# Attention stage: both query roundings ahead of both subtractions, the halves of a transposed pair laid one behind the other, reciprocal and scaling as a stage of their own

## Chip, cores and metric

The kernel runs on one core of a Trainium2 chip, in one launch. The metric is the device time of one execution in microseconds. "Before" ran three times; the median is 2232.25 us. One further execution was profiled, and the durations quoted here come from it.

## What is computed

One step of a two-layer encoder for a prompt of 1024 rows and a sample of 32 rows, with 1024 features in float32. Layer 0 is an mLSTM mixer with a SwiGLU feed-forward part, layer 1 is windowed attention with a second feed-forward part. Only the attention of layer 1 is touched by the change. Its reference, cut to what matters:

```python
def sink_attention(q, k, v, sinks, bias):
    s = jnp.einsum('bcqhgd,bckhd->bchgqk', q, k).astype(F32) * (HEAD_DIM ** -0.5) + bias
    sk = sinks.astype(F32).reshape(N_KV_HEADS, GROUP)[:, :, None, None]
    mx = jnp.maximum(jnp.max(s, -1, keepdims=True), sk)
    p = jnp.exp(s - mx)
    p = p / (jnp.sum(p, -1, keepdims=True) + jnp.exp(sk - mx))
    return jnp.einsum('bchgqk,bckhd->bcqhgd', p.astype(v.dtype), v)
```

There are 16 query heads of 64 features and 2 key/value heads. A query chunk of 64 rows sees 192 keys: its own chunk and the two before it. The sample sees 128 cached keys and its own 32. Each head has a learned sink, which enters the maximum and the sum and has no value row.

## The kernel before

**Number format.** TensorE multiplies in a rounded format. So an operand x is kept as two parts: hi, which ScalarE (ACT in the profile) makes by a rounding copy, and lo = x - hi, which VectorE (DVE) or GpSimd (POOL) makes by a subtraction. A dense product (`gemm`, L400 to L411) takes three products for each block of 128 features: hi by hi (L408), hi by lo (L409), lo by hi (L410). Dense weights are loaded by SyncE's queue, cast by ACT (L240) and subtracted by POOL or DVE (L242). The activations are split in L438 and L439, the tiles being `sx`.

**Order.** The order of issue is written out by hand. The dense products are the main thread. After each block of three products `wv.tick(us)` advances the clock of the scheduler by the estimated time of the block, and each generator whose pause has run out is pushed on to its next `yield`; what it issues then stands in the engines' queues between the dense products. `wv.drain` pushes one generator on without any dense products between. Every engine works through its own queue in order, so an instruction that has to wait holds all that is queued behind it.

**Queries.** `q_group(j, g)` (L1662) projects the query heads 2j and 2j+1 for a group g of 384, 384 or 288 columns into one PSUM bank (tile `d`; partitions 0 to 63 are one head, 64 to 127 the other). It then scales and splits them into the tile `Q`. For each half i, ACT rounds the half into its own partitions (L1677), and DVE subtracts: scaled source minus rounded value (L1678), with the result on the other 64 partitions. So in `Q` a column holds hi of a head on one half of the partitions and lo on the other. In the group of 288 columns this is done twice, for 256 and for 32 columns.

**Attention.** `attention` (L1778) goes over 72 items (j, b): 8 pairs of query heads and 9 blocks b of the sequence (8 of the prompt, 128 query rows each, and the sample as block 8). `pipeline` (L105) carries each item through stages, each of them a function with a lag and a pause:

- `scores` (L1790): four products (two in block 8) into `psS` (L1807); DVE adds the bias and takes the running minimum into the tile `s` and into `st` (L1813). Signs are turned around, so a minimum serves as the maximum.
- `soft` (L1821): ACT takes the exponential with its sum (L1828), DVE the reciprocal of the sum (L1833), POOL multiplies the probabilities by it (L1836; L1840 in the blocks 0 and 8).
- `turn` (L1850), lag 1: PE transposes the probabilities into the PSUM tile `T` (L1861); ACT rounds them into `hi` (L1865) and DVE subtracts into `lo` (L1866). Two successive items, j even and j odd, share one pair of tiles `hi`, `lo`. In blocks 0 and 8 this is done in two cuts.
- `values` (L1868), lag 1: on the odd item of a pair, up to eight products with the values into `O` (L1890).
- `place` (L1892): ACT copies the lower half of `O` (L1904) and DVE adds both halves into the activations `act` (L1908).

A stage with lag 1 takes an item only when the stage before it is two items ahead; with lag 0, one item. In each turn of its loop, `pipeline` looks at the stages in the order 4, 2, 3, 1, 0 (place, turn, values, soft, scores) and issues one item of each that may go. `turn` and `scores` pause for `GAP_A` = 0.46 us, the odd `values` for 0.92 us.

**Around it.** The first four query groups are projected while the layer normalisation before them still runs; then the values of the first group are transposed (L1762) and split (`VR`, L1691, L1692). While the attention runs, the main thread projects the other query groups; it waits with ticks of 0.25 us where the scores are too far behind (L1954). From the third column group on, it multiplies the finished part by the output weights (`out_tile`, L1237). `before(0)` (L1945) drains the attention generator up to the end of the first column group, `finish` (L1976) to its end. `mixed_parts` (L1205) splits the finished activations.

Of the kernel before, what the change touches and what calls it, by code (L numbers as in the profile page):

```python
# [9 lines left out]
F32 = mybir.dt.float32  # L10
F32R = mybir.dt.float32r
AF = mybir.ActivationFunctionType
ALU = mybir.AluOpType
# [3 lines left out]
P = 128  # L17
# [3 lines left out]
DEC = 32  # L21
# [264 lines left out]
def kernel(ctx: ExitStack, tc: tile.TileContext, A, O):  # L286
    nc = tc.nc
# [5 lines left out]
    def pool(name, space=None, side=None):  # L293
        kw = {}
        if space is not None:
            kw["space"] = space
        if side is not None:
            kw["side"] = side
        return tc.tile_pool(name=name, bufs=1, reuse_waits="tile", **kw)

    def new(p, tag, shape, dt=F32, bufs=1):
        uid[0] += 1
        return p.tile(list(shape), dt, name=f"{tag}_{uid[0]}", tag=tag, bufs=bufs)
# [20 lines left out]
    for j in range(PAIRS):  # L324
        U_Q.append(add("wqk", 2 * j))
        U_K.append(add("wqk", 2 * j + 1))
        v = ("wv", 2 * j - 2) if j else ("wvg", 0)
# [103 lines left out]
    def project(u, g):  # L431

        ps = psdense(g)
        gemm(ps, wcols(u), xcols(g))
        return ps
# [1226 lines left out]
    def q_group(j, g):  # L1662

        t0, n = GRP[g]
        ps = project(U_QB[g > 0][j], g)
        q = Q[j, g] = new(pb, "Q", [P, 2 * 384], F32R, bufs=4)
        sc = -(HD ** -0.5)
        for a, w in ((0, LC), (LC * (n // LC), n % LC)):
            m = n // LC * LC if w == LC else w
            if not m:  # L1670
                continue
            src = ps[:, a : a + m].rearrange("p (c w) -> p c w", w=w)
            dst = q[:, 2 * a : 2 * a + 2 * m].rearrange("p (c h w) -> p c h w", h=2, w=w)
            for i in range(2):
                own, other = slice(64 * i, 64 * i + 64), slice(64 - 64 * i, 128 - 64 * i)
                h = dst[own, :, i]
                nc.scalar.activation(h, src[own], AF.Copy, scale=sc)  # L1677
                nc.vector.scalar_tensor_tensor(  # L1678
                    dst[other, :, i], src[own], sc, h.bitcast(F32), op0=ALU.mult, op1=ALU.subtract
                )  # L1680

    ck = new(pb, "ck", [P, P])
# [44 lines left out]
    for j in range(4):  # L1727
        q_group(j, 0)
        W.done(U_QB[0][j])
# [13 lines left out]
    pb2 = eb.enter_context(pool("pb2"))  # L1743
# [34 lines left out]
    def attention(gap):  # L1778
        S, pairs_ = {}, {}

        def parts(b):

            if b == 0:
                return [(0, 400, 130, 64, 0, 1 + P), (1, 258, 258, P, 0, 1 + LC)]
            if b == 8:
                return [(0, 2, 2, P + DEC, SEQ, 1)]
            k0 = (b - 1) * P
            return [(0, 2, 2, WK, k0, 1), (1, 2 + WK, 2 + WK, WK, k0 + LC, 1)]
# [32 lines left out]
        def soft(j, b):  # L1821
            s = S[j, b]
            p, st = s["p"], s["st"]
            rows = 2 * DEC if b == 8 else P
            for c, _, at, nk, _, _ in parts(b):
                first = b != 0 and c == 0
                cols = slice(at - first, at + nk + (not first))
                nc.scalar.activation(  # L1828
                    p[:rows, cols], p[:rows, cols], AF.Exp, bias=st[:rows, 0, c : c + 1], scale=-1.0,
                    accum_out=st[:rows, 1, c : c + 1],  # L1830
                )
            n = len(parts(b))
            nc.vector.reciprocal(st[:rows, 2, :n], st[:rows, 1, :n])  # L1833
            if 0 < b < 8:
                w = p[:, 2 : 2 + 2 * WK].rearrange("p (c k) -> p c k", c=2)
                nc.gpsimd.tensor_mul(w, w, st[:, 2].unsqueeze(2).broadcast_to([P, 2, WK]))  # L1836
            else:
                for c, _, at, nk, _, _ in parts(b):
                    w = p[:rows, at : at + nk]
                    nc.gpsimd.tensor_scalar_mul(w, w, st[:rows, 2, c : c + 1])  # L1840

        def blocks(b):

            if b == 0:
                return [(1, 130, 64), (2, 258, P)]
            if b == 8:
                return [(0, 2, P), (1, 130, DEC)]
            return [(t, 2 + t * P, P) for t in range(3)]

        def turn(j, b):  # L1850
            s = S.pop((j, b))
            p = s["p"]
            rows = 2 * DEC if b == 8 else P
            if j % 2 == 0:
                pairs_[j // 2, b] = {
                    tag: new(pb2, tag, [P, 3, 2, P], F32R, bufs=2) for tag in ("hi", "lo")
                }
            s = pairs_[j // 2, b]
            pt = new(psb, "T", [P, 512], bufs=2).rearrange("p (t r) -> p t r", t=4)
            for t, at, nk in blocks(b):  # L1860
                nc.tensor.transpose(pt[:nk, t, :rows], p[:rows, at : at + nk], ident[:rows, :rows])  # L1861
            cuts = [(slice(0, 3), P)] if 0 < b < 8 else [(slice(t, t + 1), nk) for t, _, nk in blocks(b)]
            hi, lo = (s[x][:, :, j % 2, :] for x in ("hi", "lo"))
            for t, nk in cuts:
                nc.scalar.copy(hi[:nk, t, :rows], pt[:nk, t, :rows])  # L1865
                nc.vector.tensor_sub(lo[:nk, t, :rows], pt[:nk, t, :rows], hi[:nk, t, :rows].bitcast(F32))  # L1866

        def values(j, b):  # L1868

            if j % 2 == 0:  # L1870
                return
            s = pairs_[j // 2, b]
            g2 = j // 4
            po = s["po"] = new(psb, "O", [P, 2, 2, P])
            full = lambda i: VR[:, i, g2].rearrange("p a d -> p (a d)")
            if b == 0:
                sums = [[(1, full(0), 64)], [(2, full(0), P)]]
            elif b == 8:
                sums = [[(0, full(9), P), (1, full(8), DEC)]]
            else:  # L1880
                sums = [
                    [(0, full(b - 1), P), (1, VZ[0][:, b], P)],
                    [(1, VZ[1][:, b - 1], P), (2, full(b), P)],
                ]
            rows = 2 * DEC if b == 8 else P
            for c, terms in enumerate(sums):
                out = po[:, c, :, :rows]
                todo = [(v, s[x][:nk, t, :, :rows], nk) for t, v, nk in terms for x in ("hi", "lo")]
                for i, (v, x, nk) in enumerate(todo):
                    nc.tensor.matmul(out, v[:nk], x, start=i == 0, stop=i == len(todo) - 1)  # L1890

        def place(j, b):  # L1892
# [12 lines left out]
            for h in range(2):  # L1905
# [4 lines left out]
        always = lambda j, b: True  # L1910
# [3 lines left out]
            [  # L1914
                (scores, lambda j, b: ast["ready"] > QG.index((j, CH[b][3])), 0, (gap,) * 8),
                (soft, always, 0, 0),
                (turn, always, 1, (gap,) * 8),
                (values, lambda j, b: ast["v"] > b, 1, (0.0, 2 * gap) * 4),
                (place, always, 0, 0),
            ],  # L1920
            (4, 2, 3, 1, 0),
        )


    for t in spread:
        wv.drain(t)
    wv.launch(v_turn(0, 0))
    task = wv.launch(attention(GAP_A))
    ast["ready"] = 4
    for g in range(1, 3):  # L1930
# [20 lines left out]
    for n, (jp, g) in enumerate(JG):  # L1951
        if n < 2:
            continue
        while ast["scored"] < 6 * (n - 1):  # L1954
            wv.tick(0.25)
        for j in (2 * jp, 2 * jp + 1):
            q_group(j, g)
            wv.launch(q_made())
            if g != 1:
                W.done(U_QB[g > 0][j])  # L1960
        if n == 3:
            nparts[0] = 0
            parts = wv.launch(
                mixed_parts(
                    scr,
                    lambda g: ast["ready"] > QG.index((7, g)),
                    lambda k, g: ast["placed"] >= last_item(k, g),
                    (1.6, 1.0, 1.0),
                )
            )  # L1970
        if g == 2 and jp < EARLY:
            before(0)
            out_tile(U_OUT_B[0][jp], jp, QUARTERS[0][0])
            W.done(U_OUT_B[0][jp])
# [140 lines left out]
```

## Time and profile before

| | us |
|---|---|
| median of 3 runs (lowest, highest) | 2232.25 (2231.88, 2234.61) |
| profiled execution, device time | 2232.42 |
| its span, first to last instruction | 2230.6 |
| attention products, first to last (L1807 to L1890) | 1211.1 to 1443.9 |

The span is cut by the page into 40 slices of 55.8 us; the attention fills slices 22 to 26. A row of a group of instructions names line, engine, operation, tile written and tiles read, form and count; then the busy time, the mean of one, and the idle time of the engine ahead of them with what ended it. In the lists of waits "A <- B" says that A's engine stood idle until B had finished. PE is TensorE, PEld its weight load.

### The profile page before, as it was taken

What the parts mean: (1) busy time and instruction counts of PE and PEld (TensorE: products, weight loads), DVE (VectorE), ACT (ScalarE), POOL (GpSimd) and SP (SyncE); (2) the same over time, 40 slices, a digit from 0 to 9 for tenths busy, and PEclk for the clock granted to TensorE, in tenths of its full rate; (3) what the DMA queues carried; (4) which work ended last, traced back from release to release, by engine and by line L of the source; (5) the groups of instructions that cost most, each with busy time, mean ns of one, the idle gap of its engine ahead of it and who ended that gap; (6) DMA issues with size and microseconds to landing.
All of it is one profiled execution on the core that took longest, in us unless ns stands there. A gap on an engine that the chain in (4) does not pass through costs nothing.

```text
span 2230.6 us, 43755 instructions
## 1 busy us (share of the span) xinstructions
PE 2176.4 (98%) x16982; PEld 2143.3 (96%) x16982; DVE 1444.7 (65%) x2812; ACT 1006.7 (45%) x2263; POOL 952.6 (43%) x976
## 2 busy tenths in 40 slices
PE   9999999999999999999998989899999999999997
PEld 9999999999999999999997888799999999999997
DVE  4465677787666655566577666788765666466657
ACT  4444455374444443322246767756444444432125
POOL 2544210004655555544435645400565555554441
PEclk9999999999999999999999999999999999999999
DMA  5221213212434433896524311321344334397722
GB/s 169 77 61 56 57 39 100 75 39 97 156 144 154 145 126 125 308 303 214 162 70 124 100 57 55 99 82 39 106 165 155 138 143 155 124 338 264 236 65 78
DMA packets 166192, 289.97 MB, mean 130 GB/s; under 512 B 16416, under 2 KB 121944, under 8 KB 165984
## 3 DMA queue, kind: packets, MB, share of 16 engines
q1 hardware_dynamic: 161632, 282.84, 37.9%
q10 hardware_dynamic: 4352, 4.33, 0.6%
q8 instruction: 134, 2.20, 0.4%
q14 instruction: 74, 0.61, 0.1%
HBM read 202.35 MB, written 82.94 MB: 128 GB/s over the span
## 4 chain that ended last, share of the span: by engine, by line
PE 83%; DVE 8%; ACT 5%; DMA 2%; issue 1%; POOL 1%; SPq 0%; ACTq 0%; DVEq 0%; POOLq 0%
PE d L408 9%; PE A L408 9%; PE d L410 9%; PE A L410 9%; PE A L409 9%; PE d L409 9%; PE B L408 7%; PE B L409 7%; PE B L410 7%; PE O L1890 1%; ACT s L1828 1%; ACT act L511 1%; DVE Q L1678 1%; DMA hs_x<-z 1%; DMA sx<-hs_t 1%
## 5 line engine op out<-in xcount | busy, mean ns | idle before, releaser
L242 POOL TENSOR_TENSOR wl_s<-wr,wh_s 128x512 fp32r<-128x512 f32 x224 | 304.5, 1369 | 237.0 <-ACT wh_s L240 175.6
L408 PE MATMUL d<-sx,wh 128*128 128x264 f32 (+2 forms) x1048 | 338.4, 323 | 4.1 <-ACT wh L240 4.0
L242 POOL TENSOR_TENSOR wl_a<-wr,wh_a 128x512 fp32r<-128x512 f32 x112 | 153.3, 1372 | 413.4 <-ACT wh_a L240 409.6
L410 PE MATMUL d<-sx,wl 128*128 128x264 f32 (+2 forms) x1048 | 321.6, 307 | 4.2 <-DVE wl L242 2.8
L409 PE MATMUL d<-sx,wh 128*128 128x264 f32 (+2 forms) x1048 | 321.3, 307 | 0.4 <-DVE sx L439 0.4
L408 PE MATMUL A<-sx,wh_s 128*128 128x264 f32 x896 | 254.5, 284 | 0.0
L409 PE MATMUL A<-sx,wh_s 128*128 128x264 f32 x896 | 254.2, 284 | 0.0
L410 PE MATMUL A<-sx,wl_s 128*128 128x264 f32 x896 | 254.0, 283 | 0.0
L240 ACT CAST wh_s<-wr 128x512 fp32r<-128x512 f32 x224 | 135.7, 617 | 192.5 <-DVE wr L195 102.6
L408 PEld LDWEIGHTS d<-sx,wh 128*128 128x128 f32 x1048 | 199.5, 190 | 7.4 <-ACT wh L240 4.3
L410 PEld LDWEIGHTS d<-sx,wl 128*128 128x128 f32 x1048 | 198.8, 190 | 5.5 <-DVE wl L242 3.3
L409 PEld LDWEIGHTS d<-sx,wh 128*128 128x128 f32 x1048 | 199.8, 191 | 1.5 <-DVE sx L439 0.7
L408 PE MATMUL d<-sx,ex 128*128 128x264 f32 x624 | 180.6, 289 | 0.1
L409 PE MATMUL d<-sx,ex 128*128 128x264 f32 x624 | 177.2, 284 | 0.0
L410 PE MATMUL d<-sx,ex 128*128 128x264 f32 x624 | 176.9, 284 | 0.0
L410 PEld LDWEIGHTS A<-sx,wl_s 128*128 128x128 f32 x896 | 168.8, 188 | 0.0
L409 PEld LDWEIGHTS A<-sx,wh_s 128*128 128x128 f32 x896 | 168.4, 188 | 0.0
L408 PEld LDWEIGHTS A<-sx,wh_s 128*128 128x128 f32 x896 | 168.4, 188 | 0.0
L1335 POOL TENSOR_TENSOR z<-z 128x528 fp32r<-128x528 f32 x76 | 103.4, 1361 | 126.4 <-ACT z L1334 113.0
L242 POOL TENSOR_TENSOR wl<-wr,wh 128x512 fp32r<-128x512 f32 (+2 forms) x82 | 105.9, 1296 | 108.2 <-ACT wh L240 106.9
L408 PE MATMUL A<-ex,wh_s 128*128 128x264 f32 x448 | 127.5, 285 | 0.0
L409 PE MATMUL A<-ex,wh_s 128*128 128x264 f32 x448 | 127.1, 284 | 0.0
(359 smaller groups left out, 7193.6 us busy)
## 6 DMA issues: line engine op xcount, KB each, us to landing
wr<-in_gu SPq DMA_DIRECT2D x92, 512.0 KB, 4.8
hs_x<-z SPq DMA_DIRECT2D x72, 528.0 KB, 3.0
hs_t<-z SPq DMA_DIRECT2D x64, 528.0 KB, 2.7
sx<-hs_x SPq DMA_DIRECT2D x112, 264.0 KB, 6.0
sx<-hs_t SPq DMA_DIRECT2D x64, 264.0 KB, 6.3
ex<-hs_t SPq DMA_DIRECT2D x64, 264.0 KB, 6.7
wr<-in_dn SPq DMA_DIRECT2D x32, 512.0 KB, 3.6
ex<-hs_x SPq DMA_DIRECT2D x32, 264.0 KB, 4.9
```

Source lines behind the costliest of these rows:

```text
L240: self.nc.scalar.copy(hi, r)
L242: eng.tensor_sub(lo, r, hi.bitcast(F32))
L408: nc.tensor.matmul(out, ah, bh, start=start and k == 0, stop=False, **kw)
L409: nc.tensor.matmul(out, ah, bl, start=False, stop=False, **kw)
L410: nc.tensor.matmul(out, al, bh, start=False, stop=stop and k == last, **kw)
L511: nc.scalar.activation(z, z, AF.Identity, scale=gk, bias=bk)
L1335: eng.tensor_sub(lo.bitcast(F32R), buf(s), hi)
L1678: nc.vector.scalar_tensor_tensor(dst[other, :, i], src[own], sc, h.bitcast(F32), op0=ALU.mult, op1=ALU.subtract)
L1828: nc.scalar.activation(p[:rows, cols], p[:rows, cols], AF.Exp, bias=st[:rows, 0, c : c + 1], scale=-1.0, accum_out=st[:rows, 1, c : c + 1],)
L1890: nc.tensor.matmul(out, v[:nk], x, start=i == 0, stop=i == len(todo) - 1)
```

## The change

It changes three things in the attention stage, and no arithmetic.

1. In `q_group` both roundings (ACT) are issued first, then both subtractions (DVE). Before, they alternated: rounding, subtraction, rounding, subtraction.
2. The tiles `hi` and `lo` of a pair are laid out as [128, 2, 3, 128] instead of [128, 3, 2, 128]: the three blocks of the even item, then the three of the odd one. The products in `values` read the two halves with a gap between them.
3. Reciprocal and scaling leave `soft` and become a stage `scale` behind it, with lag 0 and no pause. The pipeline has six stages, looked at in the order 5, 3, 4, 2, 1, 0 (place, turn, values, scale, soft, scores).

```diff
@@ q_group
+            half = [slice(64 * i, 64 * i + 64) for i in range(2)]
             for i in range(2):
-                own, other = slice(64 * i, 64 * i + 64), slice(64 - 64 * i, 128 - 64 * i)
-                h = dst[own, :, i]
-                nc.scalar.activation(h, src[own], AF.Copy, scale=sc)
+                nc.scalar.activation(dst[half[i], :, i], src[half[i]], AF.Copy, scale=sc)
+            for i in range(2):
+                h = dst[half[i], :, i].bitcast(F32)
                 nc.vector.scalar_tensor_tensor(
-                    dst[other, :, i], src[own], sc, h.bitcast(F32), op0=ALU.mult, op1=ALU.subtract
+                    dst[half[1 - i], :, i], src[half[i]], sc, h, op0=ALU.mult, op1=ALU.subtract
                 )
@@ soft
+
+        def scale(j, b):
+            s = S[j, b]
+            p, st = s["p"], s["st"]
+            rows = 2 * DEC if b == 8 else P
             n = len(parts(b))
             nc.vector.reciprocal(st[:rows, 2, :n], st[:rows, 1, :n])
...
@@ turn
-                    tag: new(pb2, tag, [P, 3, 2, P], F32R, bufs=2) for tag in ("hi", "lo")
+                    tag: new(pb2, tag, [P, 2, 3, P], F32R, bufs=2) for tag in ("hi", "lo")
...
-            hi, lo = (s[x][:, :, j % 2, :] for x in ("hi", "lo"))
+            hi, lo = (s[x][:, j % 2] for x in ("hi", "lo"))
@@ values
-                todo = [(v, s[x][:nk, t, :, :rows], nk) for t, v, nk in terms for x in ("hi", "lo")]
+                todo = [(v, s[x][:nk, :, t, :rows], nk) for t, v, nk in terms for x in ("hi", "lo")]
@@ attention
                 (soft, always, 0, 0),
+                (scale, always, 0, 0),
                 (turn, always, 1, (gap,) * 8),
...
-            (4, 2, 3, 1, 0),
+            (5, 3, 4, 2, 1, 0),
```

## Prediction

> **What bounds the kernel now.** I read the page first, for the share of each engine; then the table of windows around the attention; then the list of waits there, engine by engine; then the timeline at the longest waits.
>
> ```profile
> span 2230.6 us, 43755 instructions
> ## 1 busy us (share of the span) xinstructions
> PE 2176.4 (98%) x16982; PEld 2143.3 (96%) x16982; DVE 1444.7 (65%) x2812; ACT 1006.7 (45%) x2263; POOL 952.6 (43%) x976
> ```
>
> TensorE (PE) is busy for 2176.4 of 2230.6 us, so all that can be won by a new order is the 54.2 us in which it is not, and what its clock loses. The changed lines run in three stretches of the windows table (columns: stretch, its length, busy time of PE, PE's weight load, DVE, ACT and POOL, each with its instructions, then the granted PE clock, the DMA share and GB/s):
>
> ```profile
> 1180.00:1208.00 28.00, 18.12 (x87) 16.71 (x86) 20.32 (x34) 20.17 (x42) 14.62 (x11) 0.85 0.50 157
> 1208.00:1445.00 237.00, 215.75 (x1495) 199.81 (x1494) 155.68 (x602) 165.53 (x528) 125.84 (x185) 0.97 0.25 74
> 1445.00:1452.00 7.00, 4.21 (x35) 3.96 (x33) 6.85 (x15) 5.02 (x11) 0.00 (x0) 1.00 0.71 247
> ```
>
> PE stands still for 9.9 us before the attention pipeline has filled, 21.3 us while it runs, and 2.8 us at its end: 34 of the 54 us. In the long stretch no engine is full: PE 91%, ACT 70%, DVE 66%, POOL 53%. That is the picture of engines that wait for one another in turn. What ended PE's waits, in the middle stretch and at the start (total us, times, longest):
>
> ```profile
> PE T L1861 <- POOL s L1836: 9.7, 12, 2.0
> PE O L1890 <- DVE act L1908: 6.4, 4, 1.8
> PE T L1861 <- POOL s L1840: 2.3, 5, 0.8
> ```
> ```profile
> PE T L1762 <- DVE VR L1692: 5.1, 1, 5.1
> PE d L408 <- ACT wh L240: 4.0, 1, 4.0
> ```
> So PE waits mainly for the scaled probabilities: 17 transposes, 12.0 us. The reason stands in the waits of ACT and of DVE over the whole stage:
>
> ```profile
> ACT Q L1677 <- DVE Q L1678: 29.5, 40, 2.6
> ACT hi L1865 <- DVE lo L1866: 13.4, 16, 1.8
> ```
> ```profile
> DVE st L1833 <- ACT s L1828: 27.0, 48, 1.1
> DVE Q L1678 <- ACT Q L1677: 21.4, 44, 1.4
> ```
>
> ACT loses 29.5 us with its second query rounding (call it A1) waiting for DVE's first subtraction (D0), though A1 needs nothing that D0 makes. DVE loses 27.0 us with the reciprocal at the head of its queue, waiting for the exponential issued just before it. Both put everything behind them late. One case of the timeline shows both:
>
> ```profile
> 1281.80 0.49 ACT L1677 ACTIVATE Q<-d 64x384 fp32r<-64x384 f32 x1 [1.18 <-DVE Q L1678]
> ...
> 1282.31 0.46 ACT L1828 ACTIVATE s<-s,st 128x193 f32<-128x193 f32 x1
> 1282.32 0.56 DVE L1678 SCALAR_TENSOR_TENSOR Q<-d,Q 64x384 fp32r<-64x384 f32 x1 [0.55 <-ACT Q L1677]
> ...
> 1283.33 0.17 DVE L1833 RECIPROCAL st<-st 128x2 f32<-128x2 f32 x1 [0.45 <-ACT s L1828]
> ...
> 1283.64 0.83 POOL L1836 TENSOR_TENSOR s<-s,st 128x384 f32<-128x384 f32 x1 [3.02 <-DVE st L1833]
> ...
> 1284.52 0.33 PE L1861 MATMUL T<-ident,s 128*128 128x128 f32 x1 [2.04 <-POOL s L1836]
> ```
>
> A1 is held for 1.18 us, the exponential follows it, the second subtraction and the reciprocal follow in DVE's queue, POOL has been idle for 3.02 us, and PE stands for 2.04 us at the end of it.
>
> **Query roundings (T1, T3).** Nothing is added or removed: 64 roundings and 64 subtractions keep their durations. A1 moves ahead of D0, so ACT's queue loses its hold. The chain itself gets no shorter: A0, A1, D0, D1 one after another are as long as A0, D0, A1, D1. What gains is what stands behind. At the start:
>
> ```profile
> 1192.83 0.49 ACT L1677 ACTIVATE Q<-d 64x384 fp32r<-64x384 f32 x1 [2.63 <-DVE Q L1678]
> 1193.34 0.62 ACT L240 CAST wh<-wr 128x512 fp32r<-128x512 f32 x1
> ```
> ```profile
> 1202.11 0.49 ACT L1677 ACTIVATE Q<-d 64x384 fp32r<-64x384 f32 x1 [1.13 <-DVE Q L1678]
> 1202.62 1.14 ACT L240 CAST wh<-wr 128x512 fp32r<-128x512 f32 x2
> 1203.78 0.48 ACT L1677 ACTIVATE Q<-d 64x384 fp32r<-64x384 f32 x1
> ```
> ```profile
> 1205.40 0.56 DVE L1678 SCALAR_TENSOR_TENSOR Q<-d,Q 64x384 fp32r<-64x384 f32 x1 [0.55 <-ACT Q L1677]
> ```
>
> The weight cast at 1193.34, for which PE waits 4.0 us, comes up to 2.63 us earlier. PE then only arrives sooner at its next wait, the 5.1 us for VR, whose subtraction stands behind the last query subtraction on DVE. That one ended at 1205.96. Without the 1.13 us hold of the rounding ahead of them the two casts start near 1201.5, the last A0 at 1202.64 and A1 ends at 1203.63; two subtractions of 0.56 us then end at 1204.80, 1.2 us earlier. **T1 = -1.2**, between 0 (DVE's normalisation behind it fills the time) and -2.6 (all of the first hold passes on). In the last groups of columns each query group has a second, 32-column part, so that the alternation is twice as long:
>
> ```profile
> 1290.86 0.38 ACT L1677 ACTIVATE Q<-d 64x256 fp32r<-64x256 f32 x1 [1.29 <-DVE Q L1678]
> 1291.73 0.19 ACT L1677 ACTIVATE Q<-d 64x32 fp32r<-64x32 f32 x1 [0.49 <-DVE Q L1678]
> 1292.18 0.19 ACT L1677 ACTIVATE Q<-d 64x32 fp32r<-64x32 f32 x1 [0.25 <-DVE Q L1678]
> 1292.39 0.62 ACT L240 CAST wh<-wr 128x512 fp32r<-128x512 f32 x1
> ```
>
> With A1 done before, D1 follows D0 without the 0.38 us of A1 and the two changes of engine, so the first part ends about 0.45 us earlier; the second short rounding then loses its hold of 0.25 us. The cast starts 0.7 us earlier. Behind the cast stand the copy of L1904 and then L1908, for which PE waits four times, 6.4 us. Three such places lie behind a query group of this kind: **T3 = -2.0**, between 0 and -6.4.
>
> The Trainium skill, PSUM — Partial Sum Buffer, section "PSUM bank collisions raise a hardware error", has two engines collide on one bank only inside the same 32 partitions. A1 reads partitions 64 to 127 of the bank, D0 reads 0 to 63, so by that rule neither order would have to wait; this trace shows A1 waiting all the same. If D0 needed only A0 after the change, T1 would be -1.7 and the sum 0.5 us better.
>
> **Halves of a pair one behind the other: 0.** The casts and subtractions of L1865 and L1866 keep their count and size. ACT's 13.4 us behind DVE's lo are 16 waits; the sequence blocks b = 0 and b = 8, whose two cuts are cast one after the other, occur 8 times each, which makes 16, and there the second cut still follows the first. The product now reads two runs of 128 columns instead of one of 256. Block 8 reads two separate runs of 64 already:
>
> ```profile
> 1331.97 0.22 PE L1890 MATMUL O<-hi,VR 128*128 128x128 f32 x1
> 1332.03 0.28 PE L1890 MATMUL O<-lo,VR 128*128 128x128 f32 x1
> ```
>
> It starts its successor after 0.06 us for 128 columns, so a gap in the operand costs nothing I can see. Ends: 0 to +1.
>
> **Reciprocal and scaling as a stage (T2).** 72 reciprocals, 56 multiplications and 24 block scalings keep their engines and durations, and no DMA moves. In each turn of the pipeline the scaling stays where it was before its transpose, but its exponential is now issued one item earlier: 237 us over 72 items are 3.3 us of room. DVE's reciprocal therefore finds the sum ready; behind it on DVE stand the next scores' reductions and the output sums, which come sooner too. The new tile of scores reuses the one whose transposes were issued just before; those stand ahead of its score products on PE, so no new wait arises. In the case above, D1 would follow D0 at 1281.80, the reciprocal come at 1282.4, POOL end at 1283.35 and PE start 1.1 us earlier: 2.04 becomes 0.9. Per wait the hold of the reciprocal is 27.0 / 48 = 0.56 us, and a query hold adds 0.55. The 17 waits are 0.7 us on average: those that are shorter than 0.56 go, the longer ones lose 0.56 to 1.1. I take three quarters of 12.0: **T2 = -9.0**, between -4 (half of it comes back as another late operand) and -12.
>
> **Clock (T4).** The long waits are followed by stretches at reduced clock:
>
> ```profile
> 1280.00:1290.00 10.00, 7.96 (x52) 7.73 (x52) 6.80 (x24) 6.48 (x21) 4.00 (x8) 0.83 0.35 98
> 1290.00:1300.00 10.00, 8.04 (x52) 7.63 (x50) 5.24 (x23) 5.38 (x17) 4.12 (x4) 0.83 0.15 49
> ```
>
> Each loses 17% of 10 us, 1.7 us. The first contains the 2.04 us wait that shrinks to 0.9, the second the longest wait for L1908, 1.8 us, that loses 0.7. I take the first and half of the second: **T4 = -2.5**, between 0 and -3.4.
>
> **Depth of the pipeline (T5).** An item is placed one turn later. At two places the program pushes the pipeline on without dense products between (the first `before(0)` and `finish`), one item more each; an uncovered item meets a transpose wait of 0.7 us: **T5 = +1.4**, between 0 and +6.6 (a whole item of 3.3 us twice).
>
> Sum: -1.2 - 2.0 - 9.0 - 2.5 + 1.4 = -13.3. The profiled execution took 2232.4 us, 1.8 us around its span and 0.2 above the median of the runs: **2219 us**. By the ends of the terms, without T5's far end, it is -24.4 to -2.6: 2208 to 2230.
>
> **Rivals.** *Everything goes* (0.17): the holds were 29.5 us on ACT and 27.0 on DVE, far more than PE's 21.3 us of idle time, so all ends of the terms are reached: 2208. *The clock does not come back* (0.15): the lowered stretches hang on the sum of short pauses, most of which stay; T4 = 0, 2221.5. The Trainium skill, TensorE: Matmul & The Clock Gate, section "What's actually happening", halves the clock after an idle window of about 3.4 us; by it no wait of 2.0 us costs any clock and this rival's time holds. The trace speaks against it, since 0.83 was granted with a 2.04 us wait. *The wait only moves* (0.14): ACT then DVE remain in series for each pair, PE's next operand (hi, lo, or L1908's sum) is late instead; T1 and T3 alone remain: 2229 to 2232. *The depth is not hidden* (0.09): DVE is busy for 6.85 of the last 7 us, so the last item, a turn later, pushes what PE waits for there by a whole item, as at the first hand-over: +6.6 - 1.2 gives 2237.8 if the terms of the running pipeline yield nothing; it makes the kernel slower as soon as they yield under 5.4 us. Against it stands the time of the last attention product,
>
> ```profile
> 1443.58 0.32 PE L1890 MATMUL O<-lo,VR 32*128 32x128 f32 x1
> ```
>
> after which PE still has dense products, 4.2 us of them in the 7 us up to 1452.
>
> **Chances.** Forecast 0.45, with its own range 2212 to 2226. A measurement of this kernel tells about 0.2% (4.5 us) from no change: faster 0.45 + 0.17 + 0.15 = 0.77, same 0.14, slower 0.09. The range reaches from a little beyond the full gain, 2206, into the third rival, 2231.
>
> **What would show it.** In the new profile ACT's wait for DVE at the query roundings should be near 0 except before each 32-column part; the reciprocal's wait for ACT under 5 us; T<-POOL under 4 us; PE's idle time in the middle stretch near 10 us; PE's clock 0.98 or more there. Wrong I am if T<-POOL falls and PE's idle time does not, or if the reciprocal goes on waiting for ACT.

## The result and the profile after

| | before | after |
|---|---|---|
| median of 6 runs each, us (lowest, highest) | 2231.57 (2230.3, 2234.61) | 2224.42 (2221.94, 2228.38) |
| ratio of the times, 95% interval | 1 | 0.997 [0.9957, 0.9982] |
| profiled execution, us | 2232.42 | 2221.94 |

The change makes the kernel 0.3% faster, about 7 us; the forecast was 13.3. The profiled execution of the changed kernel is the fastest of its six runs, so its trace shows too much gain rather than too little. Its page, first the span and the busy time of PE (us, share, instructions), then the same three stretches as before, in the columns of the windows table:

```profile
span 2220.1 us, 43792 instructions
...
PE 2170.3 (98%) x16982; PEld 2140.2 (96%) x16982; DVE 1441.2 (65%) x2812; ACT 1007.1 (45%) x2263; POOL 951.5 (43%) x976
```
```profile
1180.00:1208.00 28.00, 20.54 (x95) 18.50 (x94) 19.30 (x35) 20.91 (x42) 15.64 (x13) 0.85 0.50 156
1208.00:1433.00 225.00, 206.64 (x1482) 194.75 (x1481) 152.83 (x597) 163.57 (x522) 123.94 (x183) 0.99 0.26 78
1433.00:1442.00 9.00, 5.69 (x43) 5.27 (x42) 8.67 (x20) 6.84 (x16) 0.00 (x0) 1.00 0.67 198
```

The span is 10.5 us shorter: PE's idle time fell from 54.2 to 49.8 us, and its busy time by 6.1, part of which is clock (0.97 to 0.99 in the long stretch). In the long stretch PE still stands for 225.00 - 206.64 = 18.4 us, where the forecast had 10. The waits say why. First PE's own from 1208 us on, then ACT's and DVE's over the whole stage (total us, times, longest):

```profile
PE T L1867 <- POOL s L1846: 6.5, 7, 2.3
PE T L1867 <- POOL s L1842: 6.5, 7, 1.5
PE O L1896 <- DVE act L1914: 3.6, 4, 1.4
```
```profile
DVE Q L1679 <- ACT Q L1676: 17.4, 25, 1.9
DVE lo L1872 <- ACT hi L1871: 15.7, 38, 1.3
DVE s L1814 <- PE psS L1808: 14.5, 14, 2.2
DVE act L1914 <- ACT t L1910: 10.6, 17, 1.7
ACT Q L1676 <- DVE Q L1679: 9.1, 8, 1.8
```

ACT's hold has fallen to a third: it waits 9.1 us for DVE at the query roundings in place of 29.5, 8 times, each ahead of a 32-column part. DVE's has all but gone: the reciprocal's wait for the exponential fell from 27.0 us to 1.6 and is no longer among the longest. And yet the transposes wait 6.5 + 6.5 = 13.0 us for the scaled probabilities, where they waited 12.0. The place that the prediction took as its case looks like this in the changed kernel's timeline (start, us, engine, line, operation, tiles, form, idle time before it and what ended it):

```profile
1277.90 0.98 ACT L1676 ACTIVATE Q<-d 64x384 fp32r<-64x384 f32 x2
1278.91 1.12 DVE L1679 SCALAR_TENSOR_TENSOR Q<-d,Q 64x384 fp32r<-64x384 f32 x2 [0.27 <-ACT Q L1676]
1280.05 0.17 DVE L1839 RECIPROCAL st<-st 128x2 f32<-128x2 f32 x1
1280.38 0.83 POOL L1842 TENSOR_TENSOR s<-s,st 128x384 f32<-128x384 f32 x1 [2.66 <-ACT sx L438]
...
1281.27 0.33 PE L1867 MATMUL T<-ident,s 128*128 128x128 f32 x1 [1.29 <-POOL s L1842]
```

The two roundings run one after the other, and so do the two subtractions. But the reciprocal stands directly behind those subtractions in DVE's queue; it waits for nobody's result and is late all the same. The wait of 2.04 us became 1.29.

### The profile page after: what moved, and what is told of

It is laid out like the page before. It is cut to its first block, busy times and chain, and to the rows that moved or that the text cites. A ratio compares the mean times of both kernels' runs of the same rounds, so it can differ in the third digit from the quotient of the medians.

```text
span 2220.1 us, 43792 instructions
## 1 busy us (share of the span) xinstructions
PE 2170.3 (98%) x16982; PEld 2140.2 (96%) x16982; DVE 1441.2 (65%) x2812; ACT 1007.1 (45%) x2263; POOL 951.5 (43%) x976
## 4 chain that ended last, share of the span: by engine, by line
PE 84%; DVE 7%; ACT 5%; DMA 2%; issue 1%; POOL 1%; SPq 0%; ACTq 0%; DVEq 0%; POOLq 0%
PE d L408 10%; PE d L410 10%; PE d L409 10%; PE A L408 9%; PE A L410 9%; PE A L409 9%; PE B L408 7%; PE B L409 7%; PE B L410 7%; PE O L1896 1%; ACT act L511 1%; ACT s L1829 1%; ACT Q L1676 1%; PE psS L1808 1%; DMA sx<-hs_t 1%
## 5 line engine op out<-in xcount | busy, mean ns | idle before, releaser
L242 POOL TENSOR_TENSOR wl_s<-wr,wh_s 128x512 fp32r<-128x512 f32 x224 | 304.3, 1367 | 237.5 <-ACT wh_s L240 173.1
L242 POOL TENSOR_TENSOR wl_a<-wr,wh_a 128x512 fp32r<-128x512 f32 x112 | 153.4, 1372 | 412.0 <-ACT wh_a L240 409.2
L242 POOL TENSOR_TENSOR wl<-wr,wh 128x512 fp32r<-128x512 f32 (+2 forms) x82 | 105.4, 1290 | 113.5 <-ACT wh L240 102.8
```

The lines of the kernel that those rows point to most:

```text
L242: eng.tensor_sub(lo, r, hi.bitcast(F32))
```

## Experiments

Each ratio is against the kernel before on the same chip, whose medians were 2232.53, 2232.38 and 2232.17 us in the three groups. Nothing but the edit that is named differs from the kernel it starts from.

### Which part does it?

The first theory is that of the prediction: the stage for reciprocal and scaling carries most of the gain. Its rival gives it to the order of the roundings. Each part was put alone into the kernel before, and the whole change was run again beside them.

**Roundings alone.**

```diff
             for i in range(2):
-                nc.scalar.activation(h, src[own], AF.Copy, scale=sc)
-                nc.vector.scalar_tensor_tensor(...)
+                nc.scalar.activation(dst[half[i], :, i], src[half[i]], AF.Copy, scale=sc)
+            for i in range(2):
+                nc.vector.scalar_tensor_tensor(...)
```

> Before with the query roundings alone moved ahead of the subtractions. Theory 1 (both holds cost, and their gains add): about -4 us, of which -2 at the start and -3 in the running pipeline; ACT's wait for DVE at the query roundings falls from 29.5 to about 10 us, DVE's reciprocal still waits 25 us or more for ACT, and PE's wait for scaled probabilities stays between 9 and 14 us. Rival 2 (the roundings carry the whole gain, the stage gives nothing): -7 us or more. Rival 3 (the stage carries it): 0 to -2 us, at the start only.

Measured: 2218.53 us, 0.9936 [0.9924, 0.9949], 14 us faster than before and faster than the whole change. The waits of its PE, then of ACT and DVE, then the transpose of the prediction's case:

```profile
PE T L1862 <- POOL s L1837: 4.9, 9, 1.1
PE O L1891 <- DVE act L1909: 4.7, 4, 1.8
PE T L1862 <- POOL s L1841: 3.6, 5, 1.7
```
```profile
ACT Q L1676 <- DVE Q L1679: 9.2, 8, 1.3
DVE st L1834 <- ACT s L1829: 23.0, 44, 1.1
```
```profile
1280.92 0.55 PE L1862 MATMUL T<-ident,s 128*128 128x128 f32 x3 [1.08 <-POOL s L1837]
```

The hold on ACT is as small as with the whole change. The hold of the reciprocal is nearly what it was, 23.0 us after 27.0, and still the transposes wait only 8.5 us in place of 12.0. Most of that hold is therefore no longer on PE's path: of the transposes' waits 2.1 us end with a reciprocal that had waited for its exponential, where it was some 7 us in the kernel before.

**Stage alone.**

```diff
-            nc.vector.reciprocal(...)
+        def scale(j, b):
+            nc.vector.reciprocal(...)
...
+                (scale, always, 0, 0),
-            (4, 2, 3, 1, 0),
+            (5, 3, 4, 2, 1, 0),
```

> Before with the reciprocal and the scaling alone as a stage of their own. Theory 1: about -3 us; the reciprocal's wait for ACT falls from 27 us to under 2, and what ends PE's waits for scaled probabilities is now the reciprocal behind query subtractions on DVE or POOL's weight subtraction, 9 to 14 us in all. Rival 2: 0, or up to +2 by the deeper pipeline at the two hand-overs. Rival 3: -6 us or more.

Measured: 2236.51 us, 1.0016 [1.0007, 1.0024]: alone the stage makes the kernel slower, by more than any of the three expectations allowed. The waits of PE from 1208 us on, and the place of the case once more in its timeline:

```profile
PE T L1866 <- POOL s L1841: 10.5, 11, 2.4
PE T L1866 <- POOL s L1845: 7.3, 9, 2.3
...
PE O L1895 <- ACT hi L1870: 3.8, 3, 2.0
```
```profile
1284.67 0.49 ACT L1677 ACTIVATE Q<-d 64x384 fp32r<-64x384 f32 x1 [0.88 <-DVE Q L1678]
1285.19 0.56 DVE L1678 SCALAR_TENSOR_TENSOR Q<-d,Q 64x384 fp32r<-64x384 f32 x1 [0.55 <-ACT Q L1677]
1285.76 0.17 DVE L1838 RECIPROCAL st<-st 128x2 f32<-128x2 f32 x1
1286.10 0.83 POOL L1841 TENSOR_TENSOR s<-s,st 128x384 f32<-128x384 f32 x1 [2.96 <-DVE st L1838]
1286.98 0.44 PE L1866 MATMUL T<-ident,s 128*128 128x128 f32 x2 [1.70 <-POOL s L1841]
```

The transposes wait 17.8 us, half as much again as the 12.0 us in the kernel before. At the place of the case the wait fell only from 2.04 to 1.70 us: the reciprocal no longer waits for the exponential, but it could not have started before the second subtraction ended, and that one is held by the alternation, which this kernel keeps. With the roundings alone the same transpose waits 1.08 us. So most of the gain that the prediction saw at this place belongs to the roundings.

**Layout alone**: the tiles `hi` and `lo` as [P, 2, 3, P].

> Before with the halves of a pair laid one behind the other and nothing else. All theories: 0 within 2 us; the products with two runs of 128 columns still start 0.12 us apart, the casts and subtractions keep 0.475 and 0.556 us. A rival on this part alone, that a gap in the operand costs, would show 0.15 us or more between the products and up to +8 us.

Measured: 2233.68 us, 1.0007 [0.9998, 1.0016]. No difference that can be measured; the products of 256 columns start 0.118 us apart in both kernels.

**The whole change again.**

> The whole change once more on the same chip, as the mark for the parts: -5 to -10 us. If the parts add up, it equals their sum within 2 us; if it is less than the larger of them, they compete for the same idle time of PE.

Measured: 2223.95 us, 0.9966 [0.9954, 0.9978], as the first time. So the roundings carry the whole gain; the stage costs about 4 us alone, and 2223.95 - 2218.53 = 5.4 us on top of the roundings. The parts add up within the 2 us expected: -14.0 + 4.0 + 1.1 = -8.9 us, against -8.6 for the whole.

### Is the depth the stage's price?

With the stage each item is one turn longer in the pipeline. The next four ask whether depth in itself helps (theory A of the expectations) or costs (its rival), and what the place of reciprocal, scaling and subtraction does.

**Depth alone**, in the kernel before and on top of the roundings: the transposes follow one item later, with a fifth buffer of probabilities; reciprocal and scaling stay at the exponential.

```diff
-            p = s["p"] = new(pb2, "s", [P, 2 * WK + 4], bufs=4)
+            p = s["p"] = new(pb2, "s", [P, 2 * WK + 4], bufs=5)
...
-                (turn, always, 1, (gap,) * 8),
+                (turn, always, 2, (gap,) * 8),
```

> Before, with the transposes one item further behind (lag 2 for turn, five tiles of scores instead of four); roundings and reciprocal as before. It buys the same depth as the stage, but behind the scaling instead of ahead of the reciprocal. Theory A (the stage spent its depth between exponential and reciprocal, 2.3 us, where nothing waited for it; PE lacks slack between scaling and transpose): PE's waits for scaled probabilities fall from 12.0 to under 3 us, the mean slack from the end of the scaling to its transpose rises from 1.1 to over 3 us, and the time falls by 6 us or more. Rival B (depth as such costs, at the hand-overs): the waits fall, the idle time comes back elsewhere, 0 to +5 us.

> Roundings ahead of subtractions, and turn with lag 2; no stage of its own for the reciprocal. Theory A: 4 us or more below the roundings alone, near 2214 us, with PE's waits for scaled probabilities under 2 us. Rival B: at or above the roundings alone, 2218 to 2224 us.

Measured: 2234.63 us, 1.001 [1.0001, 1.0019], and 2222.39 us, 0.9953 [0.994, 0.9965]: 2 us slower than before, 4 us slower than the roundings alone. PE's waits with depth alone, and one case:

```profile
PE O L1890 <- DVE act L1908: 8.0, 7, 1.9
...
PE O L1890 <- ACT hi L1865: 3.9, 4, 1.5
...
PE O L1890 <- ACT s L1828: 1.8, 1, 1.8
PE O L1890 <- DVE lo L1866: 1.6, 5, 0.5
```
```profile
1369.93 0.49 PE L1861 MATMUL T<-ident,s 128*128 128x128 f32 x3
1370.07 0.58 ACT L1904 COPY t<-O 64x512 f32<-64x512 f32 x1
...
1371.35 0.19 ACT L1828 ACTIVATION_READ_ACCUMULATOR s<-s,st 128x1 f32 x1
...
1371.56 0.21 ACT L1865 CAST hi<-T 128x64 fp32r<-128x64 f32 x1
...
1371.83 0.33 PE L1890 MATMUL O<-hi,VR 128*128 128x128 f32 x1 [1.00 <-ACT hi L1865]
```

Not one transpose waits for POOL any more. The products with the values wait instead: their operand `hi` stands on ACT behind the copy of `O` and two exponentials, 1.14 us after the transposes have ended. This is the wait that only moves, in its clearest form: 12.0 us of one wait went, and the idle time of PE in the whole stage fell by only 3.3 us. Three more windows at half clock, some 5 us (below), took more than that back. By their times both runs lie in the range of rival B, but the products' waits are spread over the whole stage, not found at the hand-overs.

**The reciprocal behind the next item's reductions**, same depth as before, on top of the roundings: `scale` is called at the end of the next item's `scores`, or in `turn` if it has not been called by then.

```diff
             ast["scored"] += 1
+            while owed_:
+                scale(*owed_.pop(0))
```

> Roundings ahead of subtractions; reciprocal and scaling are issued right after the next item's reductions on DVE, so that the reductions run while the exponential does; same depth as before. The reciprocal's wait for ACT, 23 us with the roundings alone, should fall under 10. Theory A: that hold of DVE is not what PE waits for; within 2 us of the roundings alone. Rival C (the hold costs, and only the stage's depth spoils the gain): 3 us or more below the roundings alone.

Measured: 2233.69 us, 1.0005 [0.9997, 1.0014]. This loses all that the roundings won, 15 us, which no theory had foreseen, although the reciprocal's wait for ACT fell from 23.0 to 0.3 us. Its timeline shows one case:

```profile
1326.67 1.26 POOL L242 TENSOR_TENSOR wl<-wr,wh 128x512 fp32r<-128x512 f32 x1 [5.48 <-ACT wh L240]
...
1326.91 0.16 DVE L1842 RECIPROCAL st<-st 128x2 f32<-128x2 f32 x1
...
1327.89 1.61 POOL L1845 TENSOR_TENSOR s<-s,st 128x384 f32<-128x384 f32 x2
...
1328.77 0.48 PE L1873 MATMUL T<-ident,s 128*128 128x128 f32 x1 [3.56 <-POOL s L1845]
```

The exponential of that item had ended at 1321.92. Its reciprocal came 5 us later, behind a query group and the next item's reductions, and its scaling then met a weight subtraction on POOL. Over the stage DVE waits 25.4 us for new scores at the head of its queue (9.6 with the roundings alone) with the reciprocals of finished items behind it, and the transposes wait 17.2 us.

**The second subtraction later**, on top of the roundings: from the third pair of heads on it goes out 0.7 us of dense work after the first.

```diff
+            def later(less=less):
+                yield 0.7
+                less(1)
             less(0)
-            less(1)
+            wv.launch(later())
```

> Roundings ahead of subtractions, and the second subtraction of each query group issued 0.7 us of PE time after the first, from the third pair of heads on, so that a reciprocal can come between. With the roundings alone 3.3 of 8.5 us of PE's waits for scaled probabilities end with a reciprocal that stood behind two query subtractions (1.12 us). Theory A: these fall by half, the time by 1 to 2 us. Rival: no change, since the second subtraction then delays what stands behind it.

Measured: 2215.19 us, 0.9923 [0.9911, 0.9936], the lowest median of all. The transposes wait 4.5 + 2.3 = 6.8 us; of the 3.3 us that ended with a reciprocal behind two query subtractions 0.4 are left:

```profile
PE T L1876 <- POOL s L1851: 4.5, 7, 1.0
PE O L1905 <- DVE act L1923: 3.4, 4, 1.8
...
PE T L1876 <- POOL s L1855: 2.3, 4, 1.7
```

### Is it the reciprocal's place on DVE?

The theory now was P: the stage is dear because the reciprocal stands behind feeding work on DVE. The rivals: Q, the scaling's place on POOL; D, depth.

**Whole change, the reciprocal back in `soft`**; only POOL's scaling stays in the later stage.

```diff
         def soft(j, b):
...
+            nc.vector.reciprocal(st[:rows, 2, :n], st[:rows, 1, :n])
...
         def scale(j, b):
-            nc.vector.reciprocal(st[:rows, 2, :n], st[:rows, 1, :n])
```

> The whole change, but the reciprocal stays with the exponential; only the scaling on POOL is issued one item later. The pipeline has the same depth as in the changed kernel (2224.4). Theory P (the stage's price is the reciprocal's place on DVE: one item later it stands behind query subtractions and weight subtractions): the price of some 5 us over the roundings alone (2218.5) goes, 2215 to 2221, transposes wait for POOL at most 8.6 us. Rival Q (the price is the scaling's place on POOL, behind the weight splits): 2222 to 2227, and the transposes go on waiting some 10 us or more. Rival D (an item of depth costs by itself, through later waits of the products and the clock): 2222 to 2227 with the transposes' waits below 8 us.

Measured: 2235.67 us, 1.001 [1.0001, 1.0019], 11 us slower than the whole change and outside all three expectations. Waits of DVE over the stage, and of PE from 1208 us on:

```profile
DVE st L1834 <- ACT s L1829: 27.1, 45, 1.6
```
```profile
PE O L1896 <- DVE act L1914: 7.4, 6, 2.9
PE T L1867 <- POOL s L1842: 5.1, 5, 1.5
PE O L1896 <- ACT hi L1871: 4.6, 4, 2.0
PE T L1867 <- POOL s L1846: 4.3, 6, 2.0
```

Of P a part holds: the transposes wait 9.4 us, not 13.0. In 6.2 of these the scaling stood directly behind a weight subtraction (L242) on POOL, as Q has it. But the products now wait 12.0 us where they waited 3.9 with the whole change, as with depth alone, and the half-speed windows rose from 4 to 6.

**Whole change, second subtraction later.**

> The whole change, with the second query subtraction issued 0.7 us later. Theory P: of the 13.1 us that the transposes wait for POOL, the 5.4 us in which the reciprocal stands behind query subtractions go for the most part, so 2217 to 2220. Rival: the delay is worth the same 3.3 us as on top of the roundings alone and the reciprocal goes on standing behind something else: 2220 to 2223.

Measured: 2221.17 us, 0.9947 [0.9935, 0.996]. This lies in the rival's range. The transposes go on waiting, 12.3 us, so P is not borne out; it is not refuted either, since the edit left most of what it was to take away: what they wait for reciprocals behind query subtractions fell only from 5.4 to 3.5 us. Part of the time that went is in the products' wait for `act`, 3.6 to 0.7 us.

**Both.**

> The whole change with the reciprocal at the exponential and the second query subtraction 0.7 us later. Theory P: as the roundings alone with that delay (2215.2) or a little better for the scaling's cover, 2211 to 2216. Rivals Q and D: 2219 to 2224.

Measured: 2224.99 us, 0.997 [0.9959, 0.9981], in neither range and nearer to that of Q and D.

**Roundings alone, second subtraction 1.4 us later.**

> Roundings ahead of subtractions alone, the second subtraction issued 1.4 us later in place of 0.7 (2215.2). If the gain of the delay comes from short DVE work that passes between the two subtractions and one item's work does for that: 2214 to 2217. If more room helps more: 2210 to 2213. If the delayed subtraction itself now comes late for the scores or holds the projection's buffer: above 2218.

Measured: 2218.48 us, 0.9936 [0.9924, 0.9949], just above the bound of the third case. More room brings nothing more. The intervals of 0, 0.7 and 1.4 us of delay overlap, so that the delay helps is likely, not shown.

### All kernels in one table

For each profiled execution: what PE waited in the whole attention stage for scaled probabilities (transposes) and at the products with the values, in us, every gap of the trace counted; and the number of windows of 3.41 us at half clock. The waits and windows are those of one execution; the two rows of the whole change show how far two executions differ.

| kernel | transposes | products | half-speed windows | median us |
|---|---|---|---|---|
| before | 12.3 | 7.5 | 6 | 2232.4 |
| layout alone | 11.9 | 7.4 | 7 | 2233.7 |
| stage alone | 17.8 | 6.7 | 5 | 2236.5 |
| depth alone | 0.0 | 17.1 | 9 | 2234.6 |
| roundings alone | 8.6 | 5.6 | 3 | 2218.5 |
| roundings, depth | 1.6 | 12.6 | 7 | 2222.4 |
| roundings, reciprocal behind reductions | 17.3 | 5.6 | 9 | 2233.7 |
| roundings, second subtraction 0.7 later | 7.1 | 4.5 | 5 | 2215.2 |
| roundings, second subtraction 1.4 later | 5.4 | 4.7 | 4 | 2218.5 |
| whole change | 13.1 | 4.9 | 4 | 2224.4 |
| whole change again | 14.8 | 4.9 | 5 | 2224.0 |
| whole, reciprocal in `soft` | 9.5 | 13.4 | 6 | 2235.7 |
| whole, second subtraction 0.7 later | 12.5 | 3.0 | 2 | 2221.2 |
| whole, both | 8.3 | 9.5 | 6 | 2225.0 |

No single column orders the medians. With 1.7 us for each window (half the clock for 3.41 us) the three add up to about 28 us at most in every kernel that beats the one before, and to 30 or more in every other; within the two groups the sum does not order the medians. In both kernels with depth added between scaling and transposing, the products' wait grew, by 7 and by 10 us.

## Why the prediction was partly right

The sign and the range (2206 to 2231) held. The size was half, and the working put the gain in the wrong part. That the sum came as near as it did is luck: two errors of opposite sign nearly cancel. The roundings were booked at -3.2 us and alone measured -14.0; the stage was booked at -9.0 and measured +4.0 alone and +5.4 on top of the roundings.

- **What bounds the kernel**: right. The gain is PE's idle time in the attention and its clock: idle 33.9 to 29.1 us over the stage, and two half-speed windows less at 1.7 us each, an estimated 8.2 of the span's 10.5 us. No row places the rest.
- **T2, the stage, -9.0: the step that failed.** "DVE's reciprocal therefore finds the sum ready" came true, but the conclusion that each wait loses 0.56 us or more did not. The transposes' wait is +1.0 us with the whole change and +5.8 with the stage alone. (A slip beside it: with the 0.31 us that its own rows show from reciprocal to scaling, POOL in the prediction's case would end at 1283.54, not 1283.35, and 2.04 become 1.1, not 0.9.) Two errors are in it. The reciprocal's hold of 27.0 us was counted as time to be won back; but the roundings alone win 14 us with 23.0 us of it left, and the stage alone, which takes it away, wins nothing, since it puts the reciprocal behind other work. And the room of one item was looked for ahead of the transposes, but it lies between exponential and reciprocal. From the trace, averaged over the items in the middle, in us:

| | exponential to reciprocal | reciprocal to scaling | scaling to transposes |
|---|---|---|---|
| before | 0.09 | 0.28 | 1.05 |
| whole change | 2.31 | 0.52 | 1.33 |
| depth alone | 0.08 | 0.27 | 4.00 |

  Reciprocal and scaling are issued later, behind the feeding work that is issued meanwhile. Classed by what stood directly ahead, the transposes' waits of the whole change are in the main: the reciprocal behind query subtractions 5.4 us, behind a weight subtraction on DVE 2.3, the scaling behind a weight subtraction on POOL 3.2. With the roundings alone these were 3.3, 0 and 0.6 us, and PE's idle time over the stage was 24.3 us in place of 29.1.
- **T1 and T3, the roundings, -1.2 and -2.0**: right at the two places, far too small as a whole. From the end of the layer normalisation's last product (L486) to the third transpose of the values it takes 23.7 us in place of 26.0, with the whole change as with the roundings alone (T1 about -2.3, inside its ends); that transpose's wait for VR fell from 5.1 us to 1.3 with the whole change. The products' wait for L1908 fell from 6.4 to 4.7 with the roundings alone, to 3.6 with the whole change (T3). But the roundings alone won 14.0 us, some 12 of them behind the start: from the third transpose of the values to the last attention product it takes 224.9 us in place of 236.9. "What gains is what stands behind" was worked out only for the start and the 32-column groups, while in all groups ACT, with 20 us less of holds, can take exponentials and casts earlier; the transposes' waits that end with a late exponential fell from some 7 to 2.1 us, which fits that. The prediction had booked a part of it under T2 ("a query hold adds 0.55").
- **T4, clock, -2.5**: 6 half-speed windows became 4, 3.4 us, and 5 in the second profile of the whole change. The size was about right, and the two stretches between 1280 and 1300 us that it named are gone; but the roundings alone take 3 windows away, the stage alone 1. The rival *The clock does not come back* fell.
- **T5, depth, +1.4**: wrong in place. From the last attention product to the next layer normalisation's first it takes 8.3 us, before the change 8.2, so the hand-over costs next to nothing there; the first hand-over was not measured by itself. Where depth was added between scaling and transposing, its price lies in the running pipeline, in the products' waits; in the whole change these did not rise (4.9 us after 7.5).
- **Layout, 0**: right.
- **Rivals**: *The wait only moves* is what added depth did (transposes 12.3 to 0.0 us, products 7.5 to 17.1); with the stage the transposes kept their wait. *The depth is not hidden* had the sign of the stage alone but another mechanism. *Everything goes* fell.
- **Signs to look for**: ACT's wait and the reciprocal's wait came as written, T<-POOL (13.0 for under 4) and the idle time (18.4 for 10) did not.

Open: that the stage costs 4 to 5 us is measured; that it does so by the later place of reciprocal and scaling is read from the trace, and none of the runs takes that away by itself. Open too is why the whole change keeps the products' wait at 4.9 us, while the same depth with the reciprocal in `soft` has 13.4. The two differ in the reciprocal's place alone, so its hold of DVE may cost at the greater depth and not at the smaller. A hint is that ACT's exponentials waited 8.3 us there for DVE's minima, 5.7 in the whole change, and `hi` stands behind them on ACT; no run shows it by itself.

## What to carry to other kernels

A wait at the head of an in-order queue is worth what stands behind it and is needed next, not its length: here the change that took 20 us of holds from ACT won 14. What DVE's 27 us were worth these runs can't tell, since each edit that removed them put the reciprocal behind other work, and none of these was faster for it. Before moving an instruction to a later stage, list what the program issues in between on the same engine, since it will stand behind that. When the change has several parts, put each alone into the kernel: here one part alone beat the whole, 2218.5 against 2224.4 us.

## What the runs showed of the hardware

**The clock goes by a fixed grid.** All half-speed stretches in the attention are one, two or three windows of 3.41 us, and within one trace they begin on a grid of that step (before: at 0, 4, 27, 30 and 72 steps, to 0.001). Three windows in a row of the changed kernel, then of depth alone; the eighth column is the granted clock:

```profile
1315.55:1318.95 3.40, 1.99 (x14) 1.43 (x13) 3.04 (x13) 2.21 (x8) 1.66 (x6) 1.00 0.00 0
1318.95:1322.40 3.45, 3.45 (x17) 2.98 (x16) 0.90 (x3) 0.68 (x2) 1.06 (x2) 0.51 0.00 0
1322.40:1325.80 3.40, 3.40 (x28) 3.40 (x29) 2.20 (x10) 1.72 (x7) 0.00 (x0) 1.00 0.02 5
```
```profile
1331.90:1335.35 3.45, 2.48 (x16) 1.92 (x15) 1.21 (x8) 2.62 (x12) 2.05 (x2) 1.00 0.00 0
1335.35:1338.80 3.45, 3.45 (x18) 3.45 (x17) 2.46 (x12) 2.18 (x9) 2.85 (x3) 0.51 0.11 9
1338.80:1342.20 3.40, 3.30 (x27) 3.09 (x27) 1.80 (x6) 2.61 (x9) 0.61 (x1) 1.00 0.37 145
```

A window in which PE was busy for 1.99 of 3.40 us is followed by one at half clock; the one of depth alone had two waits of 0.52 and 0.45 us in it, no long one. Over the 14 traces of this case, each of the 44 full-speed windows beginning between 1170 and 1455 us with 1.85 us or more of idle PE was followed by a half-speed one, 10 of the 43 with 1.4 to 1.85 us, 5 of the 84 with 0.9 to 1.4, none of the 919 with less. The bounds were drawn from these same windows, and below 1.85 us the idle time alone does not decide. So a wait can cost an estimated 1.7 us more than itself (half of 3.41), depending on where the grid falls, and several short waits can do it without a long one. The Trainium skill, TensorE: Matmul & The Clock Gate, section "What's actually happening", states the free-running window of 3413 ns; the traces agree. By the same section the clock falls after an idle window; here a window a little over half idle (1.85 of 3.41 us) was enough every time.

**Two engines on one tile.** In the first timeline above DVE had been idle for 0.27 us when the second rounding ended, and only then began its subtraction of the first half, whose rounding had been done for some 0.5 us. So D0 does not need A0 alone, the case that the prediction had priced at 0.5 us more: in all 25 pairs of the changed kernel before which DVE stood idle for over 0.2 us, D0 began 0.03 us after the end of A1. The two read different halves of the partitions of `d` and write different parts of `Q`. The profile's row of D0 has it wait for a semaphore, so it is the program that keeps this order; no run shows what the chip would do without it. The 32-column parts show the same the other way round: their rounding waits 0.9 to 1.8 us for DVE's subtractions of the first part, eight times.
